# A five-step attention pipeline beside column work: queries and keys of all heads through DRAM, decode attention in two lanes

## The chip, the cores and the metric

The kernel runs on one core of a Trainium2 chip. The metric is the device time of one execution in microseconds (us). Five engines matter: TensorE (PE in the profile; its weight loads are PEld), VectorE (DVE), ScalarE (ACT), GpSimd (POOL) and SyncE (SP), which issues nearly all DMA transfers here. TensorE writes its results to PSUM banks, from which VectorE or ScalarE takes them away.

## The reference

One layer of a streaming encoder with two branches. 512 prompt tokens and 8 x 16 decode tokens go through it together, as T = 640 columns:

```python
z = x @ w_in                          # q, k, v, forget, gate | delta-net parts | two merge gates
q_a, k_a, v_a, f_a, gate_a, qkv_b, a_b, beta_b, gate_b, m_a, m_b = jnp.split(z, SPLIT_IDX, axis=-1)
logf = log_sigmoid(f_a + fox_f_bias);  c = cumsum(logf)
s = einsum('bqhd,bkhd->bhqk', q, k) * FOX_SCALE          # 8 heads of 128
p = softmax(where(visible, s + c_q - c_k, -inf))         # prompt: causal over 512
o_a = einsum('bhqk,bkhd->bqhd', p, v)                    # decode: 512 cached keys + 16 new, per request
y_a = (o_a * silu(gate_a)) @ w_out_fox
y_b = gated_delta_net(...) @ w_out_gdn
h = (sigmoid(m_a) * y_a + sigmoid(m_b) * y_b) @ w_out
x1 = layer_norm(DEEPNORM_ALPHA * x + h)
x_out = x1 + sigmoid(x1 @ w_pl_gate) * rms_norm(p_l @ w_pl_proj)
return x_out, k_a, v_a, logf, new_conv, s_new            # for both groups
```

The decode half reads a cache of 512 keys and values for each of 8 requests and 8 heads: 2.1 MB of keys and 2.1 MB of values per head.

## The kernel before

**Products.** Each float32 product is made as three matmuls of split operands (high x high, low x high, high x low), with 128x320 results: two halves of T. A *plain column* (`column`, matmuls at L396 and L397) makes one block of 128 outputs in 16 k-steps of 6 matmuls, 96 in all. A *pair* (`pair`, L474) makes two such blocks with seven products instead of eight: 168 matmuls instead of 192. It needs sums of weight blocks, which GpSimd makes ahead (`weight_sums`, loads L291, additions L295, stores L301).

**Stages.** A front of pairs makes gates, values, some merge gates and the queries and keys of the heads named in `APART`. Then `phase_fox` runs attention, which is interleaved into plain columns; then come the delta net (`phase_gdn`) and the tail. In `phase_fox` the columns are the queries and keys of heads 1, 4 and 7, and three merge-gate columns (`mcol`): 9 columns. The heads of `APART` and head 0 have their queries and keys in DRAM (`qkd`), from where SP loads them (L1529).

**Order.** The order of all instructions is made when the program is built. Lanes (Python generators) are ticked once per k-step of a column; each step of a lane emits some instructions, and a number that it yields says how many k-steps it sleeps. A model clock holds a lane back until the engines are thought to be done: `every` is on how many k-steps a lane may step, and `lead` how much early it may. Instructions run in the order of emission on each engine; TensorE is in order, so a wait of an attention matmul holds up the column behind it.

**Attention of a head** (`fox_all`). Prompt queries are four blocks of 128. Each block goes through `scores` (L754 for the first, the three matmuls L388 to L390 for the others), softmax1 (maximum, then exp on ACT at L650), softmax2 (division on DVE), transposes (L726) with a copy `pT` (L729), and products with the values (L742), in a pipeline with four slots (`flow`). The decode half, `fox_dec`, is one generator: products of the cached keys (L773) and of the new keys (L776); `xd` on DVE (L779, L780) and its softmax; transposes of the cached part (L793) with two copies into `ppad` (L795); the transpose of the new rows (L799) with a copy `pn` (L801); then products with new and cached values (L807, L813). Transposes, scores and small products share three PSUM banks in turn (`sps`, names s); one more bank (`dps`) serves the decode half; columns have four others.

**Transfers.** SP issues in order of emission: for each head the cached keys and values, four tiles of 0.5 MB each (kc, vc, L627; the next head's keys once this head's products with them are emitted), bias rows nb and nbd (L637, L639), gate sg and values vn, queries and keys, the output, and a block of column weights wr (L269) for each column. One pair of weight sums (pieces ws at L291) is made in this stage as well.

Of the kernel before, what the change touches and what calls it, by code (L numbers as in the profile page):

```python
# [9 lines left out]
F32 = mybir.dt.float32  # L10
# [42 lines left out]
class Kernel:  # L53
# [19 lines left out]
    def __init__(self, tc, ins, outs):  # L73
        self.clock, self.busy, self.wrote, self.paced = 0.0, [0.0, 0.0, 0.0], {}, False
        self.tc, self.nc, self.i, self.o = tc, tc.nc, ins, outs
        self.lanes, self.every = [], 2
        self.banks, self.read, self.nbanks = [], {}, 3
        self.now = 0
# [29 lines left out]
    def watch(self, gen):  # L108


        b = list(self.busy)
        n = next(gen) or 1
        if n == self.FREE or not self.paced:
            return max(1, abs(n)), 0.0
        t = max([y for x, y in zip(b, self.busy) if x != y] + [0.0])
        return abs(n), t + (0.25 if n > 0 else -1.5)

# [525 lines left out]
    def softmax1(self, xs, n):  # L643


        nc = self.nc
        nm = self.zt([P, 1], "nm", 6)
        nc.vector.reduce_max(out=nm, in_=xs[:, 0:n], axis=AX.X, negate=True)
        sm = self.zt([P, 1], "sm", 6)
        nc.scalar.activation(xs[:, 0:n], xs[:, 0:n], AF.Exp, bias=nm, accum_out=sm)  # L650
        return sm
# [7 lines left out]
    def fox_in(self, h, q):  # L659

        nc = self.nc
        if h == 0:
            self.load_bias(0)
# [12 lines left out]
    def fox_parts(self, x, n, tag):  # L676
# [41 lines left out]
    def fox_step(self, flow):  # L718

        nc = self.nc  # L720
        spread = weigh = None
        if flow[1]:
            h, i, (xs, _) = flow[1]
            pt = self.sps()
# [5 lines left out]
            spread = h, i, pT  # L730
        if flow[0]:
            h, i, (xs, sm) = flow[0]
            self.softmax2(xs, P * (i + 1), sm)
            weigh = flow[0]
        if flow[2]:
            h, i, pT = flow[2]
            if i == 0:
                self.og = self.zt([P, T], "og", 2)
            vn, sl = self.vn[h], slice(i * P, (i + 1) * P)
            ops = self.sps()  # L740
            for kb in range(i + 1):
                nc.tensor.matmul(ops[:, 0:P], vn[:, kb, :], pT[:, kb * P:(kb + 1) * P], start=(kb == 0), stop=(kb == i))  # L742
            nc.vector.tensor_tensor(out=self.og[:, sl], in0=ops[:, 0:P], in1=self.sg[h][:, sl], op=ALU.mult)
# [20 lines left out]
    def fox_dec(self, h, q, k):  # L764
# [24 lines left out]
        self.softmax2(xd, T, sm)  # L789
        yield -2  # L790
        pt = self.dps()
        for c in range(4):
# [8 lines left out]
        nc.scalar.copy(out=pn, in_=pt[:, 0:P])  # L801
        yield 4
        while self.outdone < h - 1:
# [417 lines left out]
    def run(self, ctx):  # L1221
# [17 lines left out]
        self.sgd = self.sgf[H:]  # L1239
        self.qkd = {(h, i): dr([P, T], F32, name=f"qkd{h}{i}") for h in (0, *self.APART) for i in range(2)}  # L1240
        self.vd = dr([5, P, 1024], F32, name="vd")
# [5 lines left out]
        self.nm = 0  # L1247
        self.outs, self.decs = self.lane(), self.lane()
        work, conv, self.ends = self.lane(), self.lane(True), self.lane()
# [34 lines left out]
    def front(self, work):  # L1284
# [217 lines left out]
    def phase_fox(self, work):  # L1502
# [5 lines left out]
        self.outdone = self.decdone = -1  # L1508
        self.heads, self.sg = {}, {}
        work["gens"].append(self.fox_all())  # L1510
        self.qkdone = [-1, -1]

        self.vn = {}
        ws = self.zt([P, 1024], "ws")
        self.sums["gens"].append(self.weight_sums([ws[:, x:x + 256] for x in range(0, 1024, 256)], slice(12, 13),
                                                  (9, 7, 5, 20)))
        for h in range(H):
            qk = []
            if h in self.BETWEEN:
                self.mcol("eacc")  # L1520
            for c in range(2):
                stored = (h, c) in self.qkd
                if not stored:
                    acc = self.column()[0]
                self.until(lambda: min(self.qkdone) >= h - 2)
                x = self.zt([P, T], "qk"[c], 2)
                qk.append(x)
                if stored:
                    nc.sync.dma_start(out=x, in_=self.qkd[h, c])  # L1529
                    continue  # L1530
                for hf in range(2):
                    sl = slice(hf * HALF, (hf + 1) * HALF)
                    if c == 0:
                        nc.scalar.mul(x[:, sl], acc[hf], FOX_SCALE)
                    else:
                        nc.scalar.copy(out=x[:, sl], in_=acc[hf])
                if c:
                    nc.sync.dma_start(out=self.o["fk"][h], in_=x)
            self.heads[h] = *qk, self.now + (9 if stored else 1)
        for _ in range(2 - len(self.BETWEEN)):  # L1540
            self.mcol("eacc")

        op, pr = [], []
        for k in range(2):
            if k == 0:
                self.until(lambda: not self.sums["gens"])
            pr.append(self.zt([P, 1024], "ws", 1, "pr")[:, 0:T] if k == 0 else self.zt([P, T], "pr"))
            nc.sync.dma_start(out=pr[k], in_=self.i["pT"][k])

        def after(s):  # L1550
            if s in (12, 14):
                self.until(lambda: self.qkdone[0] >= 6 and self.outdone >= 6 * (s // 14))
# [9 lines left out]
        self.until(lambda: not self.sums["gens"])  # L1562
        nc.sync.dma_start(out=self.sqd, in_=self.eacc)

    def mcol(self, tag, **kw):
# [210 lines left out]
    def e_evac(self, n, ps):  # L1776

        nc = self.nc
        if n == 0:

            self.until(lambda: self.decdone == 7 and not self.sums["gens"])
            self.eacc = self.zt([P, T], "eacc")
            tiles = [self.zt([P, 1024], *x, "e")[:, 0:T] for x in (("kc", 4), ("kc", 4), ("ws", 1), *[("vc", 4)] * 4)]
            self.e_tiles, self.q_tiles = tiles[0:5], tiles[5:7]
# [577 lines left out]
def _layout(a):  # L2362
# [20 lines left out]
    rest = iter(m[nf:nf + 3])  # L2383
    for h in range(1, H):
        bl += [next(rest) for _ in range(h in Kernel.BETWEEN)]
        if h not in Kernel.APART:
            bl += [bq[h], bk[h]]
    bl += rest
# [85 lines left out]
```

## Time and profile before

| what | us |
|---|---|
| median of 3 executions | 2173.64 (2171.65 to 2174.12) |
| the profiled execution, its own time | 2173.18 |
| its span (first to last instruction) | 2171.3 |
| busy in it: PE / DVE / ACT / POOL | 2149.0 / 1566.0 / 1007.3 / 401.9 |
| first matmul of the attention stage | 721.92 |
| granted TensorE clock, mean | 0.999 of full speed |

Busy times count how long instructions of an engine were under way. Matmuls overlap in the pipeline, so a matmul's own duration is longer than the distance to the next, and the distance is what counts in a sum. "x16" after a row is a number of instructions. An arrow in a row of waits names what ended the wait.

### The profile page before, as it was taken

What the parts mean: (1) busy time and instruction counts of PE and PEld (TensorE: products, weight loads), DVE (VectorE), ACT (ScalarE), POOL (GpSimd) and SP (SyncE); (2) the same over time, 40 slices, a digit from 0 to 9 for tenths busy, and PEclk for the clock granted to TensorE, in tenths of its full rate; (3) what the DMA queues carried; (4) which work ended last, traced back from release to release, by engine and by line L of the source; (5) the groups of instructions that cost most, each with busy time, mean ns of one, the idle gap of its engine ahead of it and who ended that gap; (6) DMA issues with size and microseconds to landing.
All of it is one profiled execution on the core that took longest, in us unless ns stands there. A gap on an engine that the chain in (4) does not pass through costs nothing.

```text
span 2171.3 us, 41951 instructions
## 1 busy us (share of the span) xinstructions
PE 2149.0 (99%) x15438; PEld 2082.3 (96%) x15438; DVE 1566.0 (72%) x3207; ACT 1007.3 (46%) x2213; POOL 401.9 (19%) x596
## 2 busy tenths in 40 slices
PE   9999999999999999999999999999999999999998
PEld 7799999999999998899999999999999999999998
DVE  5877776767776565566478677766757787789987
ACT  4344443443444343353655566655443343354544
POOL 0022233323330101002334333332000000021100
PEclk9999999999999999999999999999999999999999
DMA  6356656666554899869978778878567656673465
GB/s 235 101 184 202 189 182 199 198 199 194 184 180 158 276 325 344 314 199 291 241 179 199 180 188 194 189 182 248 161 229 260 209 171 202 201 276 122 153 227 173
DMA packets 240670, 452.65 MB, mean 208 GB/s; under 512 B 38920, under 2 KB 122504, under 8 KB 240464
## 3 DMA queue, kind: packets, MB, share of 16 engines
q1 hardware_dynamic: 224912, 421.64, 59.5%
q0 software_dynamic: 15552, 28.32, 8.0%
q8 instruction: 122, 2.00, 0.4%
q14 instruction: 84, 0.69, 0.1%
HBM read 353.48 MB, written 96.38 MB: 207 GB/s over the span
## 4 chain that ended last, share of the span: by engine, by line
PE 91%; DVE 3%; DMA 3%; ACT 1%; SPq 0%; issue 0%; POOL 0%; ACTq 0%; DVEq 0%; POOLq 0%
PE g L474 44%; PE g L396 18%; PE g L397 18%; PE g L440 2%; PE s L974 1%; PE s L742 1%; PE s L813 1%; PE s L773 1%; DMA ws138b<-ws 0%; PE s L440 0%; PE s L1168 0%; DMA nb<-rd 0%; DVE sx L1006 0%; DVE sx L1004 0%; PE s L726 0%
## 5 line engine op out<-in xcount | busy, mean ns | idle before, releaser
L329 ACT CAST wh<-wr 128x512 fp32r<-128x512 f32 x624 | 381.2, 619 | 288.7 <-PE g L474 109.5
L335 DVE TENSOR_TENSOR wl<-wr,wh 128x512 fp32r<-128x512 f32 x516 | 358.3, 708 | 183.5 <-ACT wh L329 173.7
L474 PE MATMUL g<-xh,wh 128*128 128x320 f32 (+1 forms) x1296 | 402.9, 311 | 2.7 <-ACT m L1278 1.6
L474 PE MATMUL g<-xl,wh 128*128 128x320 f32 (+1 forms) x1296 | 401.2, 310 | 0.6 <-DVE xl L371 0.6
L474 PE MATMUL g<-xh,wl 128*128 128x320 f32 (+1 forms) x1296 | 401.4, 310 | 0.0
L396 PE MATMUL g<-xh,wh 128*128 128x320 f32 (+1 forms) x960 | 313.0, 326 | 0.7 <-ACT wh L329 0.7
L396 PE MATMUL g<-xh,wl 128*128 128x320 f32 (+1 forms) x960 | 297.1, 309 | 0.8 <-DMA wl<-in_w 0.7
L396 PE MATMUL g<-xl,wh 128*128 128x320 f32 (+1 forms) x960 | 297.2, 310 | 0.4 <-DVE xl L371 0.4
L397 PE MATMUL g<-xh,wh 128*128 128x320 f32 x960 | 297.3, 310 | 0.0
L397 PE MATMUL g<-xl,wh 128*128 128x320 f32 x960 | 297.0, 309 | 0.0
L397 PE MATMUL g<-xh,wl 128*128 128x320 f32 x960 | 296.7, 309 | 0.0
L474 PEld LDWEIGHTS g<-xh,wh 128*128 128x128 f32 x1296 | 243.9, 188 | 4.3 <-ACT m L1278 2.1
L474 PEld LDWEIGHTS g<-xl,wh 128*128 128x128 f32 x1296 | 243.7, 188 | 1.1 <-DVE xl L371 1.1
L474 PEld LDWEIGHTS g<-xh,wl 128*128 128x128 f32 x1296 | 244.1, 188 | 0.0
L474 PE MATMUL g<-t,wh 128*128 128x320 f32 (+1 forms) x1088 | 241.4, 310 | 0.0
L335 DVE TENSOR_TENSOR wl<-sr,wh 128x512 fp32r<-128x512 f32 x200 | 147.9, 759 | 98.6 <-ACT wh L329 97.6
L295 POOL TENSOR_TENSOR ws<-ws 128x171 f32<-128x171 f32 (+2 forms) x152 | 116.7, 768 | 541.5 <-DMA ws<-in_w 535.7
L396 PEld LDWEIGHTS g<-xh,wh 128*128 128x128 f32 x960 | 180.9, 188 | 11.9 <-issue 7.1
L474 PEld LDWEIGHTS g<-t,wh 128*128 128x128 f32 x1088 | 181.9, 188 | 0.6 <-issue 0.3
L396 PEld LDWEIGHTS g<-xh,wl 128*128 128x128 f32 x960 | 180.6, 188 | 1.4 <-DMA wl<-in_w 1.0
L397 PEld LDWEIGHTS g<-xh,wh 128*128 128x128 f32 x960 | 181.0, 189 | 0.9
L396 PEld LDWEIGHTS g<-xl,wh 128*128 128x128 f32 x960 | 180.9, 188 | 1.0 <-DVE xl L371 1.0
(440 smaller groups left out, 4148.8 us busy)
## 6 DMA issues: line engine op xcount, KB each, us to landing
wr<-in_w SPq DMA_DIRECT2D x252, 512.0 KB
wl<-in_w POOLq DMA_DIRECT2D x108, 256.0 KB, 5.8
kc<-in_kc SPq DMA_DIRECT2D x32, 512.0 KB
vc<-in_vc SPq DMA_DIRECT2D x32, 512.0 KB
sr<-in_w SPq DMA_DIRECT2D x25, 512.0 KB
ws<-in_w SPq DMA_DIRECT2D x96, 128.0 KB
sb<-in_w SPq DMA_DIRECT2D x80, 128.0 KB
md<-m SPq DMA_DIRECT2D x32, 320.0 KB
```

The lines of the kernel that those rows point to most:

```text
L295: nc.gpsimd.tensor_tensor(out=o, in0=x, in1=y, op=op)
L329: nc.scalar.copy(out=hi, in_=src)
L335: nc.vector.tensor_tensor(out=lo, in0=src, in1=hi.bitcast(F32), op=ALU.subtract)
L396: nc.tensor.matmul(ps[0], whl[w], xhl[o][:, a], start=(first and x == 0), stop=(last and x == 2))
L397: nc.tensor.matmul(ps[1], whl[w], xhl[o][:, b], start=(first and x == 0), stop=(last and x == 2))
L440: nc.tensor.matmul(ps, x[:, sl], w, start=(s == 0 and n == 0), stop=(s == 15 and n == 2))
L474: nc.tensor.matmul(ps, a[:, w], b, start=(k == 0 and n == 0 and not more), stop=(k == last and n == 2), skip_group_check=True)
L742: nc.tensor.matmul(ops[:, 0:P], vn[:, kb, :], pT[:, kb * P:(kb + 1) * P], start=(kb == 0), stop=(kb == i))
L773: nc.tensor.matmul(s1[32 * j:32 * j + 32, :], self.qpad[:, 2 * j + par, :], kc[:, (j % 2) * NPT:(j % 2 + 1) * NPT], start=(par == 0), stop ...
L813: nc.tensor.matmul(od[32 * j:32 * j + 32, 0:P], self.ppad[:, c, 2 * j + par, :], vc[:, o:o + P], start=False, stop=(par == 1 and c == 3), ...
L974: nc.tensor.matmul(pp[:, o:o + 256].rearrange("p (a b) -> p a b", a=2), kq[:, 0, x], kq[:, :, x], start=True, stop=True)
```

## The change

* Heads 1, 2, 3, 6 and 7 are made as pairs in the front (one pair more), those of heads 4 and 5 as plain columns in `phase_fox`, and the result is stored to DRAM. All heads load queries and keys from there, by `load_qk`, in step 1 of the head before. Two columns fewer are made in `phase_fox`: seven.
* The pipeline has a fifth slot, with a step between softmax2 and the transposes; in `fox_step` the order is transposes, products with values, scores, softmax2.
* The decode half is cut in two generators with a lane each: `fox_dec` to the softmax, `fox_dec2` from the transposes on. `xd` has two buffers, and each of the four score blocks has its own tile.
* In this stage the lanes may step on each k-step (`every` 1) and not early (`lead` 0).
* All thirteen pairs of weight sums are made in the front. The two tiles `pr` for the projection are loaded in the last column.

```diff
-    APART = 2, 3, 5, 6
+    APART = 1, 2, 3, 6, 7
-    BETWEEN = 3, 6
+    JOBS = 4, 5, None, None
...
+    def load_qk(self, h):
+        qk = []
+        for c in range(2):
+            qk.append(self.zt([P, T], "qk"[c], 2))
+            self.nc.sync.dma_start(out=qk[c], in_=self.qkd[h, c])
+        self.heads[h] = *qk, self.clock + (7 if h else 5)
...
-        flow = [None] * 4
+        flow = [None] * 5
+        self.load_qk(0)
+        self.load_bias(0)
+        self.load_qk(1)
         for h in range(H):
-            while h not in self.heads or self.heads[h][2] > self.now or min(self.outdone, self.decdone) < h - 2:
+            while h not in self.heads or self.heads[h][2] > self.clock or min(self.outdone, self.decdone) < h - 2:
...
-                self.fox_step(flow)
-                flow[0] = h, i, self.scores(h, i, q, k, parts)
+                self.fox_step(flow, (h, i, q, k, parts))
...
                 if i == 1 and h + 1 < H:
-                    while self.qkdone[1] < h - 1:
+                    while self.qkdone[1] < h - 1 or h + 1 not in self.kept:
                         yield 1
                     self.load_bias(h + 1)
+                    if h:
+                        self.load_qk(h + 1)
...
-        flow[:] = None, weigh, spread, None
+        new = (*new[0:2], self.scores(*new)) if new else None
+        if flow[1]:
+            h, i, (xs, sm) = flow[1]
+            self.softmax2(xs, P * (i + 1), sm)
+        flow[:] = None, new, flow[1], spread, None
...
-        xs = self.zt([P, NPT], "xs", 3)
+        xs = self.zt([P, w], f"xs{i}")
...
-        xd = self.zt([P, T], "xd")
+        xd = self.zt([P, T], "xd", 2)
...
         self.softmax2(xd, T, sm)
         yield -2
+        self.decs2["gens"].append(self.fox_dec2(h, xd))
+
+    def fox_dec2(self, h, xd):
+        nc = self.nc
         pt = self.dps()
...
-        yield 4
+        yield 2
         while self.outdone < h - 1:
...
-            yield from self.weight_sums([t[:, x:x + 256] for t in ws for x in (0, 256)], slice(0, 12), (6, 4, 2))
+            yield from self.weight_sums([t[:, x:x + 256] for t in ws for x in (0, 256)], slice(0, 13), (6, 4, 2))
...
+        self.every, self.lead = 1, 0.0
...
+        todo = deque((h, c) for h in self.JOBS for c in range(1 if h is None else 2))
+
+        def job():
+            h, c = todo.popleft()
+            if h is None:
+                self.mcol("eacc")
+                return
+            acc = self.column()[0]
+            x = self.zt([P, T], "pr", 1, "qk")
...
+            nc.sync.dma_start(out=self.qkd[h, c], in_=x)
+            if c:
+                nc.sync.dma_start(out=self.o["fk"][h], in_=x)
+                self.kept.add(h)
```

Lines of the changed kernel are some ten to fourteen higher: L773 becomes L783, L776 L786, L780 L790, L793 L807, L799 L813, L801 L815, L726 L735, L742 L745, L754 L764; L388 to L390, L269, L627, L637 and L639 stay.

On PE, the place in each head where the decode half's transposes stand (cb is the identity, xd the decode scores, xs the prompt's, pT their transposed copy, vn the values, kh, kl, qh, ql the split keys and queries; s is one of the three banks). Before, head 2:

```order
L793 MATMUL s<-cb,xd 128x128 x4
L799 MATMUL s<-cb,xd 128x128
L726 MATMUL s<-cb,xs 128x128 x4
L742 MATMUL s<-pT,vn 128x128 x3
L388 MATMUL s<-kh,qh 128x256
L389 MATMUL s<-kl,qh 128x256
L390 MATMUL s<-kh,ql 128x256
```

And now, with no k-step of a column between:

```order
L807 MATMUL s<-cb,xd 128x128 x4
L813 MATMUL s<-cb,xd 128x128
L735 MATMUL s<-cb,xs_8980 128x128 x2
L745 MATMUL s<-pT,vn 128x128
L388 MATMUL s<-kh,qh 128x512
L389 MATMUL s<-kl,qh 128x512
L390 MATMUL s<-kh,ql 128x512
```

The scores of the last block moved to this place, and fewer products stand between them and the transpose of the new rows. This group of rows is the same in heads 1 to 7.

On SP, from head 0's cached keys to head 1's, before:

```order
L627 DMA kc<-in_kc 128x1024 x4
L269 DMA wr<-in_w 128x1024
L627 DMA vc<-in_vc 128x1024 x4
L291 DMA ws<-in_w 128x256 x4
L269 DMA wr<-in_w 128x1024
L637 DMA nb<-rd 128x640
L639 DMA nbd<-sfd 128x1x512
L627 DMA kc<-in_kc 128x1024 x4
```

And now:

```order
L627 DMA kc<-in_kc 128x1024 x4
L269 DMA wr<-in_w 128x1024
L627 DMA vc<-in_vc 128x1024 x4
L269 DMA wr<-in_w 128x1024
L1544 DMA qkd_193<-qk 128x640
L269 DMA wr<-in_w 128x1024
L637 DMA nb<-rd 128x640
L639 DMA nbd<-sfd 128x1x512
L627 DMA kc<-in_kc 128x1024 x4
```

The pieces ws are gone, and a store of a finished query column stands ahead of head 1's keys; ahead of the first row q and k are loaded for two heads where it was one. Counted in k-steps from the stage's first column, the products of heads 0 to 7 with their cached keys stood behind 30, 46, 62, 76, 88, 102, 116 and 132 of them, and now stand behind 25, 32, 44, 56, 67, 77, 89 and 99.

More of the change, by code (lines that the diff above doesn't have):

```diff
@@ L75, in __init__ @@
         self.tc, self.nc, self.i, self.o = tc, tc.nc, ins, outs
-        self.lanes, self.every = [], 2
+        self.lanes, self.every, self.lead = [], 2, 1.5
         self.banks, self.read, self.nbanks = [], {}, 3
@@ L115, in watch @@
         t = max([y for x, y in zip(b, self.busy) if x != y] + [0.0])
-        return abs(n), t + (0.25 if n > 0 else -1.5)
+        return abs(n), t + (0.25 if n > 0 else -self.lead)
     def lane(self, dry=False):
@@ L716, in fox_all, with fox_step @@
             yield 2
-    def fox_step(self, flow):
+    def fox_step(self, flow, new=None):
         nc = self.nc
-        spread = weigh = None
-        if flow[1]:
-            h, i, (xs, _) = flow[1]
+        spread = ops = None
+        if flow[2]:
+            h, i, (xs, _) = flow[2]
             pt = self.sps()
@@ L730, in fox_step @@
             spread = h, i, pT
[L731 to L739, printed above, removed]
+        if flow[3]:
+            h, i, pT = flow[3]
+            vn = self.vn[h]
             ops = self.sps()
@@ L1239, in run @@
         self.sgd = self.sgf[H:]
-        self.qkd = {(h, i): dr([P, T], F32, name=f"qkd{h}{i}") for h in (0, *self.APART) for i in range(2)}
+        self.qkd = {(h, i): dr([P, T], F32, name=f"qkd{h}{i}") for h in range(H) for i in range(2)}
         self.vd = dr([5, P, 1024], F32, name="vd")
@@ L1247, in run @@
         self.nm = 0
-        self.outs, self.decs = self.lane(), self.lane()
+        self.outs, self.decs2, self.decs = self.lane(), self.lane(), self.lane()
         work, conv, self.ends = self.lane(), self.lane(True), self.lane()
@@ L1513, in phase_fox @@
         self.vn = {}
[L1514 to L1519, printed above, removed]
-                self.mcol("eacc")
[L1521 to L1539, printed above, removed]
@@ L1540, in phase_fox @@
-        for _ in range(2 - len(self.BETWEEN)):
-            self.mcol("eacc")
-        op, pr = [], []
[L1544 to L1548, printed above, removed]
+        todo = deque((h, c) for h in self.JOBS for c in range(1 if h is None else 2))
+        def job():
+            h, c = todo.popleft()
+            if h is None:
+                self.mcol("eacc")
+                return
+            acc = self.column()[0]
+            x = self.zt([P, T], "pr", 1, "qk")
+            for hf in range(2):
+                sl = slice(hf * HALF, (hf + 1) * HALF)
+                if c == 0:
+                    nc.scalar.mul(x[:, sl], acc[hf], FOX_SCALE)
+                else:
+                    nc.scalar.copy(out=x[:, sl], in_=acc[hf])
+            nc.sync.dma_start(out=self.qkd[h, c], in_=x)
+            if c:
+                nc.sync.dma_start(out=self.o["fk"][h], in_=x)
+                self.kept.add(h)
@@ L1550, in after @@
+        while todo:
+            job()
+        op, pr = [], []
         def after(s):
+            if s in (4, 6):
+                self.until(lambda: min(self.qkdone) >= 6)
+                pr.append(self.zt([P, T], "nb", 2, "pr") if s == 4 else self.zt([P, T], "pr"))
+                nc.sync.dma_start(out=pr[-1], in_=self.i["pT"][s // 2 - 2])
             if s in (12, 14):
@@ L1563, in phase_fox @@
         nc.sync.dma_start(out=self.sqd, in_=self.eacc)
+        self.every, self.lead = 2, 1.5
     def mcol(self, tag, **kw):
@@ L1782, in e_evac @@
             self.eacc = self.zt([P, T], "eacc")
-            tiles = [self.zt([P, 1024], *x, "e")[:, 0:T] for x in (("kc", 4), ("kc", 4), ("ws", 1), *[("vc", 4)] * 4)]
+            tiles = [self.zt([P, 1024], *x, "e")[:, 0:T] for x in (*[("kc", 4)] * 3, *[("vc", 4)] * 4)]
             self.e_tiles, self.q_tiles = tiles[0:5], tiles[5:7]
@@ L2383, in _layout @@
     rest = iter(m[nf:nf + 3])
[L2384 to L2387, printed above, removed]
+    for h in Kernel.JOBS:
+        bl += [next(rest)] if h is None else [bq[h], bk[h]]
     bl += rest
```

11 lines of the change are left out of this document (6 added, 5 removed).

## The prediction

> **What bounds the kernel now.** I read the page's first part, then the chain of waits, then the windows over the attention stage, and last the waits of TensorE there.
>
> ```profile
> PE 2149.0 (99%) x15438; PEld 2082.3 (96%) x15438; DVE 1566.0 (72%) x3207; ACT 1007.3 (46%) x2213; POOL 401.9 (19%) x596
> PE 91%; DVE 3%; DMA 3%; ACT 1%; SPq 0%; issue 0%; POOL 0%; ACTq 0%; DVEq 0%; POOLq 0%
> 327.87 14.10 PE g L474 x96
> ```
>
> TensorE is busy for 99% of the span and is 91% of the chain that ended last. So the change is worth what it takes from TensorE's list of instructions, minus every new moment in which TensorE has to wait. The third row (the chain of waits, in order of time) prices a matmul of 128x320: 14.10 / 96 = 0.147 us. One k-step of a plain column is six of them, 0.88 us, and the column's 16 k-steps are 14.1 us.
>
> Next, the windows of 40 us (span, then busy time of PE, PEld, DVE, ACT, POOL with their counts, the granted clock, the DMA share, GB/s):
>
> ```profile
> 720.00:760.00 40.00, 39.41 (x272) 37.26 (x271) 20.83 (x46) 14.24 (x35) 5.51 (x10) 1.00 0.91 320
> 760.00:800.00 40.00, 40.00 (x392) 37.42 (x391) 27.74 (x69) 16.85 (x47) 3.94 (x6) 1.00 0.89 312
> 800.00:840.00 40.00, 40.00 (x396) 36.03 (x394) 23.26 (x57) 15.21 (x41) 3.88 (x8) 1.00 0.97 353
> 840.00:880.00 40.00, 38.71 (x332) 34.13 (x325) 26.00 (x63) 15.29 (x43) 4.57 (x8) 1.00 1.01 350
> 880.00:920.00 40.00, 39.71 (x390) 35.45 (x390) 21.87 (x57) 14.10 (x37) 0.47 (x2) 1.00 0.87 317
> ```
>
> The attention stage is the one place where the DMA engines are about as busy as TensorE (share 0.87 to 1.01). The interleaved column work is what hides the loading of the caches, and TensorE still loses little. Its waits from 715 to 1000 us (total, times, longest):
>
> ```profile
> PE s L754 <- ACT pn L801: 0.8, 1, 0.8
> PE s L388 <- ACT pn L801: 0.8, 1, 0.8
> PE s L388 <- DVE xd L780: 0.7, 2, 0.5
> PE s L754 <- ACT k L1536: 0.3, 1, 0.3
> PE s L388 <- ACT pT L729: 0.3, 1, 0.3
> ```
>
> **Term 1, one pair more.** Two plain columns (192 matmuls) leave the attention stage, and one pair (168) joins the front. The 24 matmuls fewer are 24 x 0.147 = **-3.5 us**. The pair's weight blocks need one pair of sums, which exists in both kernels and only moves to the front. It is hidden by the front's matmuls, with POOL busy for 19% of the span; without that cover the pair would wait for the load of one block, 0.52 MB at 352 GB/s (a row under term 3), 1.5 us.
>
> **Term 2, the old waits.** The five rows above add up to 2.9 us; with the refill of the pipeline behind each (about 0.1) they are worth 3.5. Softmax has a slot more between scores and transposes, and the decode half a lane of its own, so these places no longer meet. I take **-3.5 us**, bounds 0 (all return elsewhere) and -3.5.
>
> **Term 3, the start.** In the changed order head 1's products with the cached keys (L783) come after 32 k-steps of the stage, where they came after 46. Then the question is whether head 1's cached keys have landed. The queue of SP before, and what the DMA engines moved:
>
> ```profile
> 726.66 0.32 SPq L1529 DMA_DIRECT2D q<-qkd  x1
> 731.44 4.67 SPq L627 DMA_DIRECT2D kc<-in_kc  x4
> 737.62 3.33 SPq L627 DMA_DIRECT2D vc<-in_vc  x4
> 741.91 4.17 SPq L291 DMA_DIRECT2D ws<-in_w  x4
> 750.96 1.91 SPq L627 DMA_DIRECT2D kc<-in_kc  x4
> 726.60:751.00 24.40, 24.40 (x175) 23.26 (x173) 9.57 (x22) 6.95 (x17) 2.09 (x4) 1.00 0.96 339
> 740.00:750.00 10.00, 10.00 (x71) 9.60 (x73) 6.64 (x17) 4.12 (x12) 0.00 (x0) 1.00 1.03 405
> 750.00:760.00 10.00, 9.41 (x68) 7.66 (x61) 6.78 (x14) 3.85 (x10) 3.42 (x6) 1.00 1.04 352
> kc<-in_kc SPq DMA_DIRECT2D x32, 512.0 KB
> wr<-in_w SPq DMA_DIRECT2D x18, 512.0 KB
> q<-qkd SPq DMA_DIRECT2D x5, 320.0 KB
> nbd<-sfd SPq DMA_DIRECT2D x8, 256.0 KB
> ```
>
> Ahead of head 1's keys SP issued, from 726.66: q and k of head 0, nb, nbd, sg, vn, both caches of head 0, four weight blocks, four pieces ws, nb and nbd of head 1. By the sizes in the last rows (a 512 KB tile is 0.52 MB; vc is as large as kc, and nb, sg, vn and k as large as q) that is 9.3 MB, of which 24.4 us x 339 GB/s = 8.3 MB had moved by 751.0, up to 0.33 of it an older store. The change adds q and k of head 1 (0.66) and one store of a made q (0.33), and takes the pieces ws away (0.52): 9.8 MB. Left at 751.0 are 1.5 to 1.9 MB and the keys' own 2.1, so 3.6 to 4.0 MB, at 405 to 352 GB/s 8.9 to 11.4 us: the last tile lands at 759.9 to 762.4.
>
> Where TensorE stands then: the stage's first matmul starts at 721.92, and the following rows show where 34 k-steps end and what stands between.
>
> ```profile
> 721.92 0.31 PE L396 MATMUL g<-xh,wh 128*128 128x320 f32 x1
> 749.64 1.92 PE L773 MATMUL s<-kc,qpad 128*32 128x512 f32 x16
> 758.51 0.39 PE L396 MATMUL g<-xh,wh 128*128 128x320 f32 x1
> ```
>
> At 758.51, 34 k-steps (30.0 us) and 6.6 us of attention work with 0.6 of waits are done. After 32 k-steps (28.2) and the same 6.0 of attention the new order arrives at 756.1, and its 16 products would end at 758.0. With the last four waiting for the last tile they end half a microsecond behind its landing, 760.4 to 762.9. The wait is 2.4 to 4.9; I take **+3.5 us**, the middle. Bounds: 0, if packets of the keys overtake what is queued ahead, and 6.5, if all 11.9 MB moved at 339.
>
> **Term 4, the scores' bank.** All of scores, transposes, weighted values and the new rows' transpose take turns in three banks of PSUM. In the rows of order above, the scores come one or two products behind the transpose of the new rows (L813), and the third bank from it is the same one: they can't start before ACT has copied pn out (L801, now L815). Before, seven products stood between. One instance, with ACT free:
>
> ```profile
> 877.98 0.60 PE L793 MATMUL s<-cb,xd 128*128 128x128 f32 x4
> 878.42 0.27 PE L799 MATMUL s<-cb,xd 128*128 128x128 f32 x1
> 878.62 0.65 ACT L795 COPY ppad<-s 128x256 f32<-128x256 f32 x2
> 879.15 0.28 ACT L801 COPY pn<-s 128x128 f32<-128x128 f32 x1
> 879.49 0.49 PE L754 MATMUL s<-k,q 128*128 128x128 f32 x2
> ```
>
> ACT needs its two ppad copies first, so pn is copied 1.17 to 1.45 us behind the start of L793, and the scores start at 1.51. The four L793 take 0.44, so 0.11 each; in the new order they, the new rows' transpose, two transposes and one product are 8 x 0.11 = 0.88, and with the turn to another kind of product TensorE is ready at about 0.95. It waits 0.55, in heads 1 to 7: 7 x 0.55 = **+3.9 us**. Bounds: 2 (ACT's copies come quicker than here) and 5.7 (0.8 each, as in the two rows of pn among the waits).
>
> **Term 5, VectorE.** The scores' bank behind the cached keys is freed by xd (L789). In two heads a weight's low part (L335) stands before it on VectorE: two waits of the longest one shown, 0.5, are **+1.0 us**, bounds 0 and 1.4.
>
> **Term 6, the transfers.** Per head both caches (4.2 MB), q, k, sg, vn, nb, the output (0.33 each) and nbd are 6.4 MB. The heads' periods, from the chain:
>
> ```profile
> 776.36 1.85 PE s L773 x16
> 914.57 1.90 PE s L773 x16
> L396 PE MATMUL g<-xh,wh 128*128 128x320 f32 x86 | 27.8, 323 | 0.0
> ```
>
> Six heads took 138.2 us, with 86 k-steps (the count of L396 between them): 75.8 us, so 10.0 to 10.2 of attention per head. The new order has 67 k-steps between the same two (32 to 99), 11.2 a head: 9.8 + 10.15 = 20.0 us of TensorE for 7.15 MB, weights included. At 353 GB/s (the fullest window of 40 us) that takes 20.3, and the 2.0 MB of heads 4 and 5 (their q and k stored, and k once more as output) once 5.6: 7.6 us too long over six heads. At 405 (the fullest of 10 us) it takes 17.7 and nothing waits. By this the transfers sit at the edge. A wait for them overlaps the bank waits, since a head that is late leaves ACT time to copy. Beside 3.9 + 1.0 I add 0.6, so terms 4 to 6 are **+5.5 us**, bounds 2 and 9.
>
> The Trainium skill, "DMA: Bandwidth & Descriptors", section "Specifications", gives a core about 358 GB/s from memory and 435 as the engines' ceiling. By 358 a head's 7.15 MB would take 20.0 us, just TensorE's; by 435 it would take 16.4 and nothing would wait.
>
> **The sum.** -3.5 - 3.5 + 3.5 + 5.5 = +2.0 us. The profiled execution took 2173.18 (span 2171.3 and 1.9 around it), which gives 2175.2; it lies 0.46 under the median of the runs shown, so I forecast **2175.6 us**. A measurement of this kernel can't tell less than 0.2% (4.3 us) from no change: under 2169.3 is faster, over 2178.0 slower. The forecast is no change, on the slow side.
>
> **Rivals.**
> *The transfers become the bound* (slower). Place: keys of heads 2 to 7 at L783 and q, k of the next head, which are last in SP's burst. Price: 7.6 by term 6, the start's 4.9 and half the bank waits, 2, against -7.0: +7.5, so 2181.1 on the median. It decides once the sustained rate is under 357 GB/s (7.15 MB in 20.0 us). For it: the two windows at 353 and 350. Against: 405 over 10 us. Chance 0.22.
>
> *The waits don't come* (faster). The keys of head 1 land by 759, and ACT finds pn early: -7.0 + 2 = -5.0, so 2168.6. For it: 405 GB/s in the stretch ahead of those keys. Against: the seven places that have the same order. Chance 0.22.
>
> *Bank waits alone*: -7.0 + 4.9 = -2.1, so 2171.5. Chance 0.11.
>
> *The clock.* One window shows what a longer gap does:
>
> ```profile
> 1440.00:1480.00 40.00, 37.42 (x275) 35.33 (x276) 31.65 (x106) 23.14 (x69) 12.39 (x21) 0.96 0.75 182
> ```
>
> With 2.6 us of gaps the granted clock was 0.96, so 4% of 40 us, 1.6 us, was lost beside the gap. In my sum it is nothing, as head 1's four key tiles land one by one with products between. If they come as one block it adds 1.6 to the first rival: 2183.
> The Trainium skill, "TensorE: Matmul & The Clock Gate", section "Part 1: The HAM clock gate", ties a halved clock to an idle window of some 3.4 us, and term 3 is about that long.
>
> **How the numbers follow.** The forecast (0.45) has its own range, 2172 to 2180. Adding rivals until 2 in 10 are left out gives 2166 to 2184. Faster: most of the second rival, 0.20. Slower: nearly all of the first and the upper third of the forecast, 0.35. Within 0.2%: 0.45.
>
> **What would show it.** Term 3: a wait at the second L783, released by DMA kc, of 2.4 to 4.9. Term 4: waits of L388 on ACT pn L815, some seven of 0.4 to 0.8. Term 2: nothing on pT at scores. Term 6: windows at 350 GB/s or more through the stage, and few waits on DMA after head 1. I am wrong if L783's waits exceed 8 us, or if pn releases TensorE for less than 2.

## The result and the profile after

The changed kernel takes 2184.12 us (median of 6, 2182.53 to 2187.09) against 2173.88 before: the ratio is 1.0051, 95% interval 1.0038 to 1.0064. It is slower by 10 us; the forecast was +2 with a range that ends 0.1 us below the median. The profiled execution took 2186.33, with a span of 2184.2.

The changed kernel's first part and chain by engine:

```profile
PE 2153.1 (99%) x15414; PEld 2083.0 (95%) x15414; DVE 1578.1 (72%) x3222; ACT 1013.6 (46%) x2219; POOL 407.6 (19%) x596
PE 88%; DMA 6%; DVE 3%; ACT 1%; SPq 1%; issue 1%; POOL 0%; ACTq 0%; POOLq 0%; DVEq 0%
```

TensorE has 24 matmuls fewer and is busy for 4 us longer. The share of DMA in the chain that ended last has doubled, from 3% to 6%. TensorE's waits in the attention stage (740 to 980 us) are three kinds:

```profile
PE s L388 <- ACT pn L815: 3.8, 8, 1.3
PE s L783 <- DMA kc<-in_kc: 3.7, 1, 3.7
PE s L764 <- DMA k<-qkd: 3.0, 3, 1.1
```

None of the kinds of before is left but pn, and the two rows on DMA are new. The windows of the stage, as before:

```profile
760.00:800.00 40.00, 34.99 (x264) 28.48 (x266) 22.09 (x53) 13.97 (x37) 0.95 (x2) 0.96 0.92 339
800.00:840.00 40.00, 38.26 (x403) 33.29 (x392) 23.96 (x62) 14.94 (x42) 0.83 (x4) 1.00 0.93 329
840.00:880.00 40.00, 37.30 (x371) 33.21 (x373) 25.21 (x66) 16.64 (x46) 0.83 (x4) 1.00 1.01 364
880.00:920.00 40.00, 39.29 (x390) 35.48 (x378) 27.10 (x69) 17.63 (x48) 0.83 (x4) 1.00 0.98 354
```

TensorE is without work for 5.0 us in the first of them, and its clock is 0.96 there.

**The stage's length** is the measure for what follows, since whole times of one kernel differ by 3 to 10 us between executions. It runs from the first column matmul to the first product of the projection, here in the timeline of the changed kernel and of the kernel before (whose stage starts at 721.92):

```profile
746.67 0.31 PE L396 MATMUL g<-xh,wh 128*128 128x320 f32 x1
985.08 0.48 PE L1817 MATMUL s<-re,cb 128*32 128x160 f32 x8
977.14 0.48 PE L1810 MATMUL s<-re,cb 128*32 128x160 f32 x8
```

It starts 24.75 us later, which is the pair in the front (168 x 0.147). Before, the stage took 255.2 us; without the two columns (32 k-steps, 28.2 us) that is 227.0, and without the old waits (3.5 with the refill behind each, from the distances of the matmuls' starts) 223.5. The changed kernel's stage is 238.4, so 14.9 us of new waits. With the refill they are: 6.6 at head 1's keys (8.8 us from the last column matmul ahead to the next one behind, for 2.2 us of products), 4.4 on pn (1.4 at head 0 and 0.44 in each of heads 1 to 7), and 3.5 at q and k, in all 14.5. At the projection the kernel is 7.9 us behind: -3.5 - 3.5 + 14.5 = +7.5. Some expectations below put the old waits at 4.0 and those on pn at 5.1: they take 0.11 us as the distance between two starts where nothing is waited for, and the run with pn copied first shows 0.19 at the places of pn.

### The profile page after: what moved, and what is told of

Same layout as the page of the kernel before. It is cut to its first block, busy times and chain, and to the rows that moved or that the text cites. A ratio compares the mean times of both kernels' runs of the same rounds, so it can differ in the third digit from the quotient of the medians.

```text
span 2184.2 us, 41964 instructions
## 1 busy us (share of the span) xinstructions
PE 2153.1 (99%) x15414; PEld 2083.0 (95%) x15414; DVE 1578.1 (72%) x3222; ACT 1013.6 (46%) x2219; POOL 407.6 (19%) x596
## 4 chain that ended last, share of the span: by engine, by line
PE 88%; DMA 6%; DVE 3%; ACT 1%; SPq 1%; issue 1%; POOL 0%; ACTq 0%; POOLq 0%; DVEq 0%
PE g L474 45%; PE g L396 17%; PE g L397 17%; PE g L440 2%; DMA k<-qkd 1%; PE s L988 1%; DMA wr<-in_w 1%; PE s L783 1%; PE s L745 1%; DMA ws138b<-ws 1%; DMA kc<-in_kc 0%; DMA vc<-in_vc 0%; PE s L440 0%; PE s L1182 0%; PE s L827 0%
## 5 line engine op out<-in xcount | busy, mean ns | idle before, releaser
L397 PE MATMUL g<-xh,wh 128*128 128x320 f32 x928 | 288.3, 311 | 0.0
L397 PE MATMUL g<-xl,wh 128*128 128x320 f32 x928 | 287.9, 310 | 0.0
L397 PE MATMUL g<-xh,wl 128*128 128x320 f32 x928 | 287.5, 310 | 0.0
L474 PEld LDWEIGHTS g<-xl,wh 128*128 128x128 f32 x1328 | 249.7, 188 | 1.1 <-DVE xl L371 1.1
L335 DVE TENSOR_TENSOR wl<-sr,wh 128x512 fp32r<-128x512 f32 x208 | 154.9, 765 | 102.1 <-ACT wh L329 101.0
L295 POOL TENSOR_TENSOR ws<-ws 128x171 f32<-128x171 f32 (+2 forms) x140 | 105.6, 754 | 518.5 <-DMA ws<-in_w 513.5
L329 ACT CAST wh<-sr 128x512 fp32r<-128x512 f32 x208 | 124.8, 618 | 133.9 <-PE g L474 104.1
```

Source lines behind the costliest of these rows:

```text
L295: nc.gpsimd.tensor_tensor(out=o, in0=x, in1=y, op=op)
L329: nc.scalar.copy(out=hi, in_=src)
L335: nc.vector.tensor_tensor(out=lo, in0=src, in1=hi.bitcast(F32), op=ALU.subtract)
L397: nc.tensor.matmul(ps[1], whl[w], xhl[o][:, b], start=(first and x == 0), stop=(last and x == 2))
L474: nc.tensor.matmul(ps, a[:, w], b, start=(k == 0 and n == 0 and not more), stop=(k == last and n == 2), skip_group_check=True)
```

## The experiments

Stage and later part come from one profiled execution each; median and ratio are those of all executions, and each ratio is taken against executions of the kernel before that were made beside it. "Later part" is from the first product of the projection to the last matmul. The two profiled executions of the changed kernel differ by 1.1 us in the stage, so a difference of about 1 us is read by comparing the starts of the matmuls one by one.

| kernel | stage, us | later part, us | median, us | ratio to before, 95% interval |
|---|---|---|---|---|
| before | 255.2 | 1185.9 | 2173.88 | 1 |
| changed | 238.4 | 1191.4 | 2184.12 | 1.0038 to 1.0064 |
| changed, again | 239.5 | 1188.4 | 2183.73 | 1.0035 to 1.0065 |
| head 1 later | 234.2 | 1187.2 | 2179.91 | 1.0018 to 1.0041 |
| pn first | 237.3 | 1185.7 | 2182.17 | 1.0034 to 1.0060 |
| q and k earlier | 235.3 | 1187.7 | 2177.89 | 1.0015 to 1.0037 |
| the three together | 229.2 | 1188.9 | 2171.74 | 0.9985 to 1.0003 |
| one head's caches | 228.5 | 1187.5 | 2172.52 | 0.9989 to 1.0007 |
| one head's caches, pn first | 226.3 | 1186.8 | 2169.05 | 0.9970 to 0.9989 |
| old pipeline | 237.9 | 1185.8 | 2180.33 | 1.0022 to 1.0050 |
| three, head 2 by 5 | 225.8 | 1201.6 | 2184.45 | 1.0047 to 1.0074 |
| three, head 2 by 4 | 226.1 | 1186.5 | 2168.76 | 0.9974 to 0.9991 |
| the same, pn as changed | 227.7 | 1185.8 | 2171.16 | 0.9986 to 1.0004 |
| before, pn first | 253.9 | 1185.6 | 2172.84 | 0.9990 to 1.0007 |

### One wait at a time

The rival to "three single waits" was a queue that is full throughout, in which a wait removed at one head turns up at the next.

*Head 1 later*: its products with the cached keys sleep 8 k-steps.

```diff
         if h == 0:
             yield 8
+        elif h == 1:
+            yield 8
         s1 = self.dps()
```

> The changed kernel, with head 1's products with the cached keys held back by 8 k-steps (40 instead of 32). Theory of single waits: the 8.8 us that TensorE spends at this place in the changed kernel, where the 16 products need 2.2, go away whole, wait and slow clock together: 6.6 us less, so about 2177.5, the granted clock 1.00 from 760 to 800 us, and no later head waits for its cached keys. Theory of a queue that is full throughout: the transfers set the end of the stage, so the wait turns up again at the keys of heads 2 to 4 or at their queries, and the time stays within 1.5 us of 2184.

The stage lost 4.2 us of 6.6. TensorE's waits in it, by the changed lines (L785 is L783 of the changed kernel):

```profile
PE s L764 <- DMA k<-qkd: 2.7, 2, 2.4
PE s L388 <- ACT pn L817: 2.1, 5, 0.5
PE s L785 <- DMA kc<-in_kc: 1.6, 3, 1.1
```

The 6.6 us at head 1's keys are gone, and as much turned up: 4.0 at head 2's keys, whose tiles land one by one (the row shows only 1.6 of them, as TensorE is at work between the tiles), and 2.5 at head 3's q and k. The gain comes from the others: the waits at q and k of heads 2, 4 and 5 (3.5) and three of the eight on pn don't come. Neither theory had that: there is a backlog from the start of the stage, and it outlives one head.

*pn first*: only ScalarE's order changes. The lines of pn (its transpose, its tile and its copy) go ahead of the two copies into ppad.

```diff
+        p2 = self.sps()
+        nc.tensor.transpose(p2[:, 0:P], xd[:, NPT:T], self.ident)
+        pn = self.zt([P, P], "sq", 2, "pn")
+        nc.scalar.copy(out=pn, in_=p2[:, 0:P])
         for par in range(2):
             nc.scalar.copy(
...
-        pt = self.sps()
-        nc.tensor.transpose(pt[:, 0:P], xd[:, NPT:T], self.ident)
-        pn = self.zt([P, P], "sq", 2, "pn")
-        nc.scalar.copy(out=pn, in_=pt[:, 0:P])
```

> The changed kernel, with ScalarE copying pn (the new rows' transpose) ahead of the two copies into ppad instead of behind them; TensorE's order is the same. Theory of single waits: the waits of L388 on pn (with what the pipeline needs to refill 5.1 us in the changed kernel) shrink to below 1 us, about 2179.5. Theory of a full queue: the heads come to their queries and keys earlier and wait there for the same time, less than 1.5 us gained.

The full queue's theory holds here: the stage is 1.2 us shorter. Matmul by matmul, the edit took 3.6 us off the places of pn, and 2.4 came back at q and k. In the rows the waits on pn fell from 3.8 to 0.7, and those for k rose from 3.0 to 5.1:

```profile
PE s L764 <- DMA k<-qkd: 5.1, 4, 2.3
PE s L783 <- DMA kc<-in_kc: 3.7, 1, 3.7
PE s L388 <- ACT pn L811: 0.7, 1, 0.7
```

*q and k earlier*: the load of the next head's q and k at the start of a head, ahead of the next cached keys.

```diff
             parts = None
+            if 0 < h < H - 1 and h + 1 in self.kept and self.qkdone[1] >= h - 1:
+                self.load_qk(h + 1)
             for i in range(4):
...
                     self.load_bias(h + 1)
-                    if h:
+                    if h and h + 1 not in self.heads:
                         self.load_qk(h + 1)
```

> The changed kernel, with the next head's q and k loaded at the start of a head (for head 5 where they were, since they are not made by then), so ahead of the next cached keys in SP's queue instead of behind them, nb and nbd. Theory of a place in the queue: the waits of L764 on k of heads 2 and 4 go (1.1 us each with refill), that of head 5 stays, 2.2 us less, about 2182, and no wait for cached keys comes instead. Theory of a full queue: 0.66 MB earlier for q and k is 0.66 MB later for the cached keys, 1.8 us at 360 GB/s, so waits at L783 take the place of those at L764 and the time stays within 1 us of 2184.

The place in the queue decides: 3.1 us less, all waits on k are gone (that of head 5 too), and no later head waits for its cached keys:

```profile
PE s L785 <- DMA kc<-in_kc: 4.0, 1, 4.0
PE s L388 <- ACT pn L817: 3.8, 8, 1.3
```

TensorE's order of matmuls is unchanged; only the order in SP's queue differs. So from head 2 on the transfers as a whole were not too slow; q and k stood too far behind.

*The three together*:

> The three edits together. Theory of single waits: they add up, 6.6 + 4.6 + 2.2 = 13.4 us less than the changed kernel, about 2170.7, that is 3 us less than before, near the 3.5 of the pair. Theory of a full queue: the heads run up against the transfers, 7.15 MB per head at 350 to 360 GB/s, and no less than half of the 13.4 us comes back as waits at L783 or L764: 2177 or more.

The stage lost 9.2 us and the median 12.4, to 2171.7. So some 70% of the sum of 13.4 came in the stage. Two waits are left: one on pn at head 0, and one at head 2's keys, which arrive one by one 7 k-steps after head 1's (3.5 us by the starts, of which the row shows 0.9):

```profile
PE s L787 <- DMA kc<-in_kc: 0.9, 2, 0.6
PE s L388 <- ACT pn L815: 0.9, 1, 0.9
```

### The transfers taken away

```diff
     def load_kv(self, h, what, j):
         store, t = (self.kc, "kc") if what == "k" else (self.vc, "vc")
+        if h:
+            store[h, j] = store[0, j]
+            return
```

> The changed kernel, with only head 0's cached keys and values loaded; the products of heads 1 to 7 take head 0's tiles, so 29 MB of transfers and the decode results of these heads are left out. The stage's length is from its first column matmul to the first product of the projection: 238.4 us in the changed kernel, 255.2 before, which without the two columns is 227.0. Theory of a full queue behind two of three waits: the 6.6 us at head 1's keys and the 3.5 at q and k go, the waits on pn stay, 0.52 each with refill in seven heads, so 227.0 - 4.0 (the waits of the kernel before, which the new order lacks) + 4 = 227 to 229. Theory that the order itself costs, whatever is transferred: 233 or more.

The stage was 228.5, in the range of the first theory. The only waits left are those on pn, 8 as before:

```profile
PE s L388 <- ACT pn L818: 4.1, 8, 1.5
800.00:840.00 40.00, 39.23 (x386) 34.62 (x385) 25.85 (x67) 16.41 (x45) 0.96 (x4) 1.00 0.49 158
```

With 158 GB/s instead of 329 the keys, q and k are never late, by the same order of instructions. So two of the three waits, 10 of 15 us, are due to transfers, and the third is not.

> The run before (one head's caches loaded, the rest left out) with pn copied ahead of the copies into ppad. It gained 1.2 us of the stage where the queue was full, against rows of waits of 5.1. Theory that the freed time went into waiting for q and k: here, with the queue empty, the same edit takes 3.5 to 4.5 us off the stage. Theory that the waits on pn were overstated by the rows: 1 to 2 us again.

The same edit took 2.2 us off the stage here, between the two theories. Matmul by matmul it took 3.6 off the places of pn, as in the full queue, and one new wait gave 1.5 back. Head 0's transposes of the decode half need the one bank out of which VectorE takes head 1's products with the cached keys (L792), and VectorE was late: it had stood for head 1's bias row nb, a transfer, which was in time in the run before:

```profile
781.24 0.35 DVE L772 SCALAR_TENSOR_TENSOR xs<-nb,colT,s 128x128 f32<-128x128 f32 x1 [1.43 <-DMA nb<-rd]
PE s L810 <- DVE xd L792: 1.4, 1, 1.4
PE s L388 <- ACT pn L814: 1.0, 1, 1.0
```

The 3.6 are the lower end of the first theory.

### The pair without the new pipeline

The flow of four slots, `fox_step` and one `fox_dec` from the kernel before, `every` 2 and `lead` 1.5, in the changed kernel.

> The changed kernel with the pipeline of before: four slots, decode half in one generator, the old pace (lanes step every second k-step). The pair and the way of all heads through DRAM stay. By the order of instructions head 1's keys are needed after 46 k-steps, as before, and the columns hold at the 101st until six heads are through. Theory: no wait for keys at head 1 and none for q and k, since the heads are 14 steps apart, but two heads run without columns beside them, each some 22 us of steps for 10 us of work, so 10 to 20 us of gaps and clock loss near the end of the stage: 2180 to 2192. Theory that the pair alone brings its 3.5 us and the pipeline isn't needed for it: 2170.

The stage was 237.9 and the median 2180.3, the first theory's lower end. No cached key was late, but from 888.0 to 916.6 the heads ran without columns beside them, and there each wait stands open (the two longest of the stage, and the window 880 to 920, whose clock of 0.83 is a loss of 6.8 us):

```profile
PE s L752 <- DMA vn<-vd: 3.2, 1, 3.2
PE s L752 <- ACT pT L739: 2.0, 1, 2.0
880.00:920.00 40.00, 34.07 (x317) 27.84 (x316) 23.03 (x61) 14.94 (x44) 0.95 (x4) 0.83 0.87 286
```

So the pair alone does not bring its 3.5 us. Both paces pay here for the two columns that left: the old one with too little cover at the end, the new one with loads that are late at the start.

### A version that beats both, and one that came late

Head 2's products were held back as well, by 5 k-steps:

```diff
-        if h == 0:
+        if h in (0, 1):
             yield 8
+        elif h == 2:
+            yield 5
```

> The three edits together (head 1's keys at 40 k-steps, pn copied first, q and k loaded earlier), and head 2's products held back by 5 more k-steps (52 instead of 47). With the three edits the stage is 229.2 us, and head 2's keys arrive one by one over 3.1 us. Theory of a backlog from the start of the stage that is worked off by then: these 3.1 us go, the stage is 226 us and the time about 2168.7. Theory of a full queue throughout: the same wait turns up at head 3, the stage stays at 229 and the time at 2171 to 2172.

The stage did what the backlog's theory said, 225.8 us. But the later part took 1201.6. TensorE is idle there for 13.0 us, where the other kernels have 5.4 to 8.0. Of its three longest rows of waits (985 us to the end) the first is in no other kernel, the other two are shorter there:

```profile
PE s L1214 <- DVE rp L1210: 2.7, 2, 2.1
PE g L396 <- DMA wl<-in_w: 2.6, 1, 2.6
PE g L474 <- DVE fx L483: 1.8, 2, 1.2
```

The order that the scheduler makes of the later stages depends on where its lanes stand when attention ends. With 5 the projection's first product stands behind 157 k-steps, not 158, and the order of TensorE's matmuls differs from 1095.6 us to 1642, deep into the delta net; with 4 it is that of the changed kernel.

> The three edits together and head 2's products held back by 4 k-steps (51 instead of 47), not 5 as in the run that ended late; with 4, TensorE's order from the projection on is that of the changed kernel, with 5 it was another. Theory that the late run lost its 13 us by that other order: the stage is 226 to 227 us as there, the later part 1186 to 1189 us, the time about 2169, 0.2% under the kernel before. Theory that spacing the heads harms the later stages in itself (transfers that come later): the later part is again over 1195 and the time over 2178.

With 4: stage 226.1, later part 1186.5, 2168.76 us, ratio 0.9983 (0.9974 to 0.9991). It is faster than both kernels, than the one before by 0.17%, with an interval that leaves out 1. TensorE waits for no transfer in the stage; the row on issue, at head 3's keys, ended 0.1 us behind ScalarE's copy out of the decode bank:

```profile
PE s L388 <- ACT pn L815: 0.9, 1, 0.9
PE s L787 <- issue: 0.5, 1, 0.5
PE s L388 <- DVE xd L794: 0.3, 1, 0.3
PE s L388 <- ACT pT L740: 0.3, 1, 0.3
```

> The spaced version (head 1's products at 40 k-steps, head 2's at 51, q and k earlier), with pn copied behind the copies into ppad again, as in the changed kernel; TensorE's order is that of the spaced version. It shows what the waits on pn cost where no transfer is late. Theory of single waits: eight waits of 0.5 to 0.6 come back, the stage is 3.5 to 4.5 us longer than 226.1 and the time 2172 to 2173, the gain over the kernel before gone. Theory that the rows overstate them, since a copy that is waited for here is waited for elsewhere otherwise (as in the run that gained 1.2 us): 1 to 2 us, 2170 to 2171.

Taking pn first out again cost 1.6 us of the stage, the second theory, with five waits of 0.4: at three of the eight places nothing waits any more. By the intervals the two can't be told apart from runs alone.

> The kernel before, with pn copied ahead of the copies into ppad. Theory of single waits: its two waits on pn, 0.98 us each with refill, go: the stage 253.3 instead of 255.2 us, the time 2 us less. Theory that they pass on to the next wait, as most of it did in the changed kernel with its full queue: under 0.7 us less.

In the kernel before the same edit took 1.4 us off the stage, between the theories, 1.1 of it at the two waits on pn; the runs show no difference (0.9990 to 1.0007).

### The changed kernel once more

> The changed kernel itself, unaltered, to have it on the chip of the other two and to see its later stages once more. The stage was 11.4 us longer than without waits, and with the 3.5 of the pair and 4.0 of old waits that makes 7.9 us more than before at the first product of the projection; from there to the end the profiled execution took 1191.4 us against 1185.9 before, while the other kernels with the same order there took 1185.7 to 1188.9. Theory that the later part differs between executions alone: 1186 to 1189 now, and a median near 2182. Theory that the change makes the later part slower: 1190 or more, and a median of 2184 or more.

The median is 2183.7 and the later part 1188.4, the stage 239.5. So 8 to 9 of the 10 us are the stage's, less the pair. Of the rest, 2.5 us in this execution and 5.5 in the first, no order of matmuls is a cause: TensorE's order in the later part is the same in all kernels but "three, head 2 by 5", the kernel before included, up to seven small products that start within 0.1 us of one another. What differs is idle time and clock. The traces record stretches of 3.4 us at half the granted clock, and one of them costs about 1.6 us (last section). In all thirteen traces of this order the later part, less TensorE's idle time (waits of 0.15 us and more) and 1.6 us for each such stretch, is 1178.2 to 1179.1. The kernel before has 5.7 us of idle time and one stretch, the changed kernel 8.0 and three, then 8.0 and one: these are the 5.5 and the 2.5. Whether the 2.3 us of idle time come from the change stays open; the variants of it have 5.4 to 7.8.

## Why the prediction was wrong

**Term 1** (one pair more, -3.5): right; 24.75 us more in the front for 28.2 fewer in the stage, by one execution each (the stage starts at 745.5 to 747.6 in the twelve executions with the pair, at 720.7 and 721.9 in the two without).

**Term 2** (old waits, -3.5): right. Those on xd, k and pT are gone.

**Term 3** (head 1's keys, +3.5, 2.4 to 4.9): the mechanism was right, its size was not: 6.6. TensorE arrived 34.0 us into the stage (780.62), where 34.2 had been worked out. The keys were late by more. The SP queue, the windows of DMA and TensorE's row in the changed kernel:

```profile
773.78 3.76 SPq L627 DMA_DIRECT2D kc<-in_kc  x4
778.49 0.33 SPq L663 DMA_DIRECT2D sg<-sgf  x1
780.38 0.38 SPq L633 DMA_DIRECT2D vn<-vd  x1
781.45 0.81 SPq L269 DMA_DIRECT2D wr<-in_w  x1
751.35:775.75 24.40, 24.37 (x169) 22.41 (x168) 12.03 (x28) 7.32 (x19) 2.86 (x6) 1.00 0.97 354
775.75:788.40 12.65, 8.95 (x52) 5.56 (x50) 5.73 (x15) 3.50 (x10) 0.00 (x0) 0.87 1.02 341
784.63 4.80 PE L783 MATMUL s<-kc,qpad 128*32 128x512 f32 x16 [3.70 <-DMA kc<-in_kc]
```

The last four products start at 788.4. Up to there 8.6 + 4.3 = 12.9 MB had moved, and I had counted 11.9 up to the keys' last byte. The missing 1 MB is what SP issued 1 to 4 us behind the keys, which I took to come after them. The trace's records of single packets tell the loads apart by their size: from 783.4 to 788.4 the packets of 512 bytes (vn) carried 0.29 MB and those of 2560 bytes (sg) 0.32, and those of 4096 bytes are 0.44 MB more than all caches and weight blocks up to the keys. At 341 GB/s this 1.05 MB takes 3.1 us, which is the whole miss. The rate was the second error, and a small one: 341 GB/s, under the 352 that I took as the lower end, is 0.4 us more on 4.3 MB. The clock, which I put at nothing since the four tiles land one by one, was rightly put so: it was 0.87 over this window, but from the first start to the last the 16 products took 4.2 us, and at head 2's keys in "head 1 later" and "the three together", with tiles that land one by one too and the clock at 1.00, they took 4.2 as well. My upper bound of 6.5 for this term doesn't come out of its own numbers: 11.9 MB at 339 GB/s, with or without the older store, give 4.3 to 5.2.

The rate has a low place that I did not see. From 778.35 to 782.35 it was 278 GB/s, where packets of nbd (2048 bytes) move, against 404 from 761.35 to 775.35. In the changed kernel's stage, the microseconds with more than 0.02 MB of nbd carried 300 GB/s on average and the others 388 (before: 284 and 383), with the DMA engines busy for 95% or more in both kinds. No run takes nbd away, so that it is the cause is not shown.

**Term 4** (pn, +3.9, up to 5.7): place, cause and number of heads right. Heads 1 to 7 took 0.44 each, 3.1 in all, where 0.55 each had been worked out; an eighth wait, at head 0, 1.4 us, was not foreseen, so 4.4. But as a gain to be had by taking the waits away it is too high a figure. The edit took 3.6 us off these places with the queue full and with one head's caches alike, and the stage gained 1.2 and 2.2: the rest passed on to the next thing that was late. In the spaced version, with five of the eight places left, it gained 1.6.

**Term 5** (VectorE, +1.0): didn't come.

**Term 6** (transfers, +0.6): mis-sized and put in the wrong place; 3.5. I asked whether 7.15 MB fit into a head's 20 us, and they did: in the spaced version (head 2 by 4) three windows of 40 us show 371 to 382 GB/s, 18 to 29 above the fullest one before (the fourth, 840 to 880, shows 356), and TensorE waits for no transfer.

```profile
760.00:800.00 40.00, 38.81 (x323) 34.20 (x323) 23.50 (x58) 14.32 (x39) 1.42 (x4) 1.00 1.04 378
800.00:840.00 40.00, 39.25 (x391) 35.18 (x389) 25.98 (x66) 17.91 (x48) 0.98 (x4) 1.00 1.02 371
880.00:920.00 40.00, 40.00 (x396) 35.64 (x394) 28.13 (x73) 17.66 (x48) 0.83 (x4) 1.00 1.01 382
```

The question that counted was another: how long the last load of a burst waits behind the others, and when it is needed. I had named q and k as last in the burst, in the slower rival, and priced them by the rate alone. The Trainium skill, "DMA: Bandwidth & Descriptors", section "Specifications", gives 358 GB/s per core; these three windows are above it.

**The slower rival** was nearest (2181), and by half for its reason: the price of 7.6 for a rate too low over six heads didn't exist, while the price of places in the queue did. The forecast's sum missed 3.1 at term 3, 2.9 at term 6 and 0.5 at term 4, less 1.0 at term 5: 5.5 of the 8.5 us between forecast and median. So the steps that failed are two sizes: what moves ahead of head 1's keys (term 3), and the time that q and k stand behind other loads (term 6). The rest fits the later part, which the forecast took as unchanged and which was 2.5 and 5.5 us longer in the two profiled executions.

## What to carry to other kernels

A stage that is made denser needs its loads earlier, and the first heads show it first: work out, for each load, what is queued ahead of it and shortly behind it and when its consumer arrives, rather than bytes per period over rate. Waits in series hide one another, so one edit alone shows a fraction (1.2 of 3.6 us) or passes its wait on; judge such edits together, and on the length of the stage that they touch. Where a scheduler sets the order, compare the order of the stages that were not edited: one k-step at the end of attention cost 15 us later on.

## What the runs showed of the hardware

A short wait of TensorE can cost more than itself. In the changed kernel a wait of 2.1 us for a weight block is followed by matmuls at 0.27 us distance instead of 0.147, and the granted clock is 0.73 over 5 us:

```profile
1052.75 0.41 PE L396 MATMUL g<-xh,wl 128*128 128x320 f32 x1 [2.10 <-DMA wl<-in_w]
1054.91 0.47 PE L396 MATMUL g<-xh,wl 128*128 128x320 f32 x1
1055.17 0.47 PE L397 MATMUL g<-xh,wl 128*128 128x320 f32 x1
1055.00:1060.00 5.00, 5.00 (x28) 5.00 (x27) 3.47 (x22) 1.95 (x4) 0.00 (x0) 0.73 1.03 244
```

From 1052.75 to the end of the slow stretch TensorE fell back by another 1.6 us (24 distances in 5.17 us, 3.53 at 0.147), beside the wait's own length. The Trainium skill, "TensorE: Matmul & The Clock Gate", section "Part 1: The HAM clock gate", speaks of an idle window of about 3.4 us; here 2.1 us were enough.

The length of the wait alone does not decide. The second execution of the changed kernel has two waits of 1.80 us; the clock fell behind the first and not behind the second:

```profile
856.19 0.35 PE L764 MATMUL s<-k,q 128*128 128x128 f32 x1 [1.80 <-DMA k<-qkd]
857.00:862.00 5.00, 5.00 (x27) 1.88 (x26) 3.22 (x9) 1.42 (x4) 0.00 (x0) 0.66 0.97 343
1052.37 0.41 PE L396 MATMUL g<-xh,wl 128*128 128x320 f32 x1 [1.80 <-DMA wl<-in_w]
1053.00:1058.00 5.00, 5.00 (x36) 5.00 (x35) 4.52 (x20) 3.64 (x7) 0.86 (x1) 1.00 1.10 277
```

In the fourteen traces 24 waits of TensorE were 1.80 to 2.75 us long, and 12 of them were followed within 4 us by a stretch at half the clock; of those from 0.9 to 1.79 us none was. What decides between two equal waits is not shown by these runs.
